# Written order for the transfer queue behind a router, and a new interleaving of two token tiles

## The chip, the cores and the metric

The kernel runs on one core of a Trainium2 chip. The metric is the device time of one execution in microseconds (us). Engines that work beside each other are PE (TensorE, matrix products), DVE (VectorE), ACT (ScalarE), POOL (GpSimd) and SP (SyncE), which here issues nearly all transfers. An engine executes its instructions in the order in which they stand in its queue; a wait of one holds up those behind it. Transfers that SP has issued are carried out by 16 DMA engines.

## What is computed

One layer on 256 tokens of 1024 values: two kinds of attention on the same modulated input, merged by sigmoid gates, an output projection, a layer norm, then a mixture of 32 experts of which each token uses four, and a second layer norm. Cut to the part around the change:

```python
x = layer_norm(DEEPNORM_ALPHA * x + gate1 * (merged @ w_out[l]), ln1_g[l], ln1_b[l])
h = x * (1.0 + scale2) + shift2
logits = jnp.dot(xt, w_router) + b_router
top_val, top_idx = lax.top_k(logits, TOP_K)
top_w = jax.nn.softmax(top_val, axis=-1)
# for each expert e, on the tokens that chose it:
g = jnp.minimum(xb @ w_gate[e] + b_gate[e], SWIGLU_LIMIT)
up = jnp.clip(xb @ w_up[e] + b_up[e], -SWIGLU_LIMIT, SWIGLU_LIMIT)
y = ((up + 1.0) * (g * jax.nn.sigmoid(SWIGLU_ALPHA * g))) @ w_down[e] + b_down[e]
x = layer_norm(DEEPNORM_ALPHA * x + gate2 * f, ln2_g[l], ln2_b[l])
```

Each expert has three weight matrices of 1024 x 1024 f32 (4 MB each), and all 32 are read.

## The kernel before

The tokens lie in two tiles (t = 0, 1) of 128; a row of 1024 values is worked on in two halves (hf = 0, 1). After attention and merging, the part around the change is the output projection and the router, written as one hand-ordered section (`order_cm`, all engines but POOL): inside it each engine executes in the order of the source.

The steps of that section: `o_part(t, hf, i)` is half i of the output projection for tile t and half hf, 12 matmuls (each product in three terms); `resid` adds the residual on DVE and takes statistics; `r_T` transposes on PE and copies on ACT; `logits(t, hf)` adds eight matmuls to the router's logits; `mod_sums` makes the column sums `gsum` and `bsum` (one PE product with `wrsum`, two DVE operations), which `route` needs; `stats` makes mean and inverse deviation; `normalise(t, hf)` writes the normalised tile `xn`; `route(t)` takes the four best experts and writes `mask_bf`; `count(t)` counts on PE each expert's tokens up to each token; `place(t)` makes from that the selection matrix `pt0` of the first experts; `gather_first(t)` gathers their tokens by 8 matmuls per tile into two PSUM banks (tile sxg), which `evacuate` copies to SBUF; `weigh` makes the weights of the four experts.

Behind it stands a second section (`pe_cm`), hand-ordered for PE alone; the order of all other engines, SP among them, is a planner's, which works with a timeline of its own. In it `expert_group` runs 14 times: first group s, with two fixed experts (30 and 31), then e0 to e12, which hold the other 30 experts sorted by how many tokens chose them (two experts each in e0 to e3 and e8 to e12, three each in e4 to e7). A group makes gate (tiles sg, e0g, ...), up (su, e0u, ...) and down (sd, e0d, ...), each in eight steps k. Inside group s, `sort_a`, `sort_b` and `sort_c` sort the experts and write their numbers to `order_i`. At the head of each of e0 to e12, `nc.sync.value_load(order_i[...])` (L1442) loads the numbers of its experts into SP's registers, two or three loads, with which the addresses of that group's weights are made.

Space sets when a transfer can be issued. The 24 weight pieces of the fixed experts (1 MB each, L805) go to 20 blocks; `al` hands out the block that was given back longest ago. 11 of the 24 are issued in the first section, 13 by `fixed_w` in group s. Then 18 of the blocks become 9 pairs of 2 MB (`open_pairs`, in the order of `PLACES`: blocks 10 and 8, 1 and 2, 0 and 12, 13 and 16, 11 and 7, 4 and 14, 5 and 15, 6 and 9, 17 and 3), and each transfer of e0 to e12 (L1126) takes the pair that was given back longest ago. `give_back` follows every second step k of a product. By `al` and `fr`, the fixed gate's last quarter lies in blocks 10 and 8; the four quarters of up lie in 1 and 2, 0 and 12, 13 and 16, 11 and 7; the first quarter of down in 4 and 14, and its last piece in block 3, which held the fixed gate's third quarter.

Of the kernel before, what the change touches and what calls it, by code (L numbers as in the profile page):

```python
# [13 lines left out]
AF = mybir.ActivationFunctionType  # L14
ALU = mybir.AluOpType
# [58 lines left out]
def tile_layer(  # L74
# [31 lines left out]
    V, A, G, T, SP = nc.vector, nc.scalar, nc.gpsimd, nc.tensor, nc.sync  # L106
# [26 lines left out]
    def al(dt=F32, stay=False):  # L133

        some = [i for i in freed if i in STAY] if stay else []
        some = some or [i for i in freed if stay_open[0] or i not in STAY]
        assert some, "no block is free"
        i = min(some, key=freed.get)
        del freed[i]
        clock[0] += 1  # L140
        v = first.pop(i, None)
        if v is None or dt != F32:
            v = (aw if i in STAY else ar).tile([P, BLK], dt, tag=f"blk{i}", bufs=1, name=f"blk{i}_{clock[0]}")
        return v, i

    def fr(*blocks):
        for i in blocks:
            clock[0] += 1
            assert i not in freed
            freed[i] = clock[0]  # L150

    def ps_a(name):
        return ps_t("A", 4, name)

    def ps_b(name):
        return ps_t("B", nb[0], name)
# [5 lines left out]
    def rsqrt_neg(v, eps, pool, name):  # L162

        y = pool.tile([P, 1], F32, tag="rsy", bufs=2, name=f"{name}y")
        u = pool.tile([P, 1], F32, tag="rsu", bufs=2, name=f"{name}u")
        V.tensor_scalar_add(v, v, eps)
        V.tensor_scalar(y.bitcast(I32), v.bitcast(I32), -0.5, 1597463007.0, op0=ALU.mult, op1=ALU.add)
        for c3 in (3.0, 12.0, 768.0):
            V.scalar_tensor_tensor(u, y, v, y, op0=ALU.mult, op1=ALU.mult)
            V.scalar_tensor_tensor(y, u, c3, y, op0=ALU.subtract, op1=ALU.mult)  # L170
        return y
# [103 lines left out]
    for j in range(4):  # L275
        ps = ps_b(f"xT{j}")
        for kk in range(2):
            for t in range(2):
                k = 2 * j + kk
# [4 lines left out]
    def mm3(o, sh, sl, mh, ml, first, last):  # L284
        T.matmul(o, sh, mh, start=first, stop=False)  # L285
        T.matmul(o, sh, ml, start=False, stop=False)  # L286
        T.matmul(o, sl, mh, start=False, stop=last)  # L287
# [406 lines left out]
    for i in range(4):  # L694
        ahead(2)
        if i % 2 == 0:
            v, r = al()
# [81 lines left out]
    def mod_sums():  # L779
        ps = ps_b("gb")  # L780
        T.matmul(ps[:, 0:2 * E], ones_p, wrsum, start=True, stop=True)
        V.tensor_copy(gsum, ps[:, 0:E])
        V.tensor_add(bsum, ps[:, E:2 * E], br_b)


    engines = {e.engine for e in (T, A, V, G, SP)}
# [12 lines left out]
    def load_fixed(n):  # L799

        for _ in range(n):
            kind, kq, j = fixed_todo.pop(0)
            v, r = al(stay=kind == 0)
            v = v.rearrange("p (k n) -> p k n", k=2)
            SP.dma_start(v, rows_of(weights[kind], E - 2 + j)[:, 2 * kq:2 * kq + 2, :])  # L805
            fixed[kind][0][j].append(v)
            fixed[kind][1][j].append(r)
# [73 lines left out]
    st6, mv, y3, lgps = [], [], [], []  # L881
# [2 lines left out]
        st6.append(p3.tile([P, 4, 6], F32, tag="lnst", bufs=2, name=f"ln1st{t}"))  # L884
    po = {}

    def o_part(t, hf, i):
        ts = slice(t * P, (t + 1) * P)
        if i == 0:
            po[t, hf] = ps_a(f"o{t}_{hf}")  # L890
        hi, lo = WO[2 * hf + i][0:2]
        for kk in range(4):
            k = 4 * i + kk
            mm3(po[t, hf], mgh[:, k, ts], mgl[:, k, ts], hi[:, kk, :], lo[:, kk, :], k == 0, k == 7)

    def resid(t, hf):
        for q in range(2):
            sl = slice(hf * 512 + q * 256, hf * 512 + (q + 1) * 256)
            V.tensor_mul(r[:, t, sl], po[t, hf][:, q * 256:(q + 1) * 256], gate1[:, sl])
            V.scalar_tensor_tensor(r[:, t, sl], x_sb[:, t, sl], ALPHA, r[:, t, sl], op0=ALU.mult, op1=ALU.add)  # L900
        for q in range(2):
            sl = slice(hf * 512 + q * 256, hf * 512 + (q + 1) * 256)
            V.bn_stats(st6[t][:, 2 * hf + q, :], r[:, t, sl])

    def r_T(t, hf):
        for q in range(2):
            ps = ps_b(f"rT{t}_{hf}_{q}")
            k = 4 * hf + 2 * q
            for kk in range(2):
                T.transpose(ps[:, kk * P:(kk + 1) * P], r[:, t, (k + kk) * P:(k + kk + 1) * P], ident)  # L910
            A.copy(rT[:, k:k + 2, :].rearrange("p a n -> p (a n)"), ps[:, 0:2 * P])

    def logits(t, hf):
        if hf == 0:
            lgps.append(ps_b(f"lg{t}"))
        for k in range(4 * hf, 4 * hf + 4):
            T.matmul(lgps[t][:, 0:E], rT[:, k, :], wrs[:, k, 0, :], start=(k == 0), stop=(k == 7))

    def stats(t):
        m = p3.tile([P, 2], F32, tag="lnmv", bufs=2, name=f"ln1mv{t}")  # L920
        V.bn_aggr(m, st6[t])
        mv.append(m)
        y3.append(rsqrt_neg(m[:, 1:2], LN_EPS, p3, f"ln1rs{t}"))
        nb_ = p3.tile([P, 1], F32, tag="lnnb", bufs=2, name=f"lnnb{t}")
        V.tensor_scalar(nb_, m[:, 0:1], y3[t], -1.0, op0=ALU.mult, op1=ALU.mult)
        nbs.append(nb_)

    nbs = []

    def normalise(t, hf):  # L930
        v = xn[:, t, :, :].rearrange("p k q -> p q k")[:, 64 * hf:64 * hf + 64, :]
        src = r[:, t, hf * 512:(hf + 1) * 512].rearrange("p (q k) -> p q k", k=8)
        if t == 0 or hf == 1:
            A.activation(v, src, AF.Identity, bias=nbs[t], scale=y3[t])
        else:
            V.tensor_scalar(v, src, y3[t], nbs[t], op0=ALU.mult, op1=ALU.add)

    m8s, ohs = [], []

    def route(t):  # L940
        lg = p3.tile([P, E], F32, tag="lg", bufs=2, name=f"lgs{t}")
        V.scalar_tensor_tensor(lg, gsum, mv[t][:, 0:1], lgps[t][:, 0:E], op0=ALU.mult, op1=ALU.subtract)
        V.scalar_tensor_tensor(lg, lg, y3[t], bsum, op0=ALU.mult, op1=ALU.add)
        m8 = p3.tile([P, 8], F32, tag="m8", bufs=2, name=f"m8_{t}")
        V.max(m8, lg)
        i8 = p3.tile([P, 8], U32, tag="i8", bufs=2, name=f"i8_{t}")
        V.max_index(i8, m8, lg)
        oh = p3.tile([P, 4, E], F32, tag="oh", bufs=2, name=f"oh{t}")
        V.tensor_tensor(oh, iota_e.unsqueeze(1).to_broadcast([P, 4, E]),
                        i8[:, 0:4].unsqueeze(2).to_broadcast([P, 4, E]), op=ALU.is_equal)  # L950
        V.tensor_reduce(mask_bf[:, t, :], oh.rearrange("p j e -> p e j"), axis=AX.X, op=ALU.max)
        m8s.append(m8)
        ohs.append(oh)
# [3 lines left out]
    def count(t):  # L957
        cum[t] = ps_b(f"cum{t}")
        if t == 1:
            T.matmul(cum[t][:, 0:E], ones_bf, mask_bf[:, 0, :], start=True, stop=False)  # L960
        T.matmul(cum[t][:, 0:E], tri, mask_bf[:, t, :], start=(t == 0), stop=True)

    def place(t):
        V.tensor_mul(posm[:, t, :], cum[t][:, 0:E], mask_bf[:, t, :])
        V.tensor_tensor(pt0[:, t, :].rearrange("p (a n) -> p a n", a=2),
                        iota_s[:, 0:CAP].unsqueeze(1).to_broadcast([P, 2, CAP]),
                        posm[:, t, E - 2:E].unsqueeze(2).to_broadcast([P, 2, CAP]), op=ALU.is_equal)
# [31 lines left out]
            else:  # L999
                V.tensor_scalar(xg[:, k, :], src, gc[:, k:k + 1], bc[:, k:k + 1], op0=ALU.mult, op1=ALU.add)  # L1000

    def gather_first(t):
        if t == 0:
            for i in range(2):
                gps.append(ps_a(f"sxg{i}"))
                T.matmul(gps[i], zero_bf, zero_bf.unsqueeze(1).to_broadcast([P, 4, P]), start=True, stop=False, skip_group_check=True)
        for k in range(8):
            T.matmul(gps[k // 4][:, (k % 4) * P:(k % 4 + 1) * P], xn[:, t, k, :], pt0[:, t, :], start=False, stop=(t == 1),
                     skip_group_check=True)

# [4 lines left out]
    for i in range(2):  # L1015
        for t in range(2):
            o_part(t, 0, i)
        fr(*WO[i][2:4])
        if i == 0:
            split_wo()  # L1020
        else:
            mod_sums()
        load_fixed(2)
    for t in range(2):
        resid(t, 0)
# [1 line left out]
        o_part(0, 1, i)  # L1027
    r_T(0, 0)
    logits(0, 0)
    resid(0, 1)  # L1030
    o_part(1, 1, 0)
    fr(*WO[2][2:4])
# [3 lines left out]
    stats(0)  # L1036
    for hf in range(2):
        normalise(0, hf)
    o_part(1, 1, 1)
    fr(*WO[3][2:4])  # L1040
    route(0)
    count(0)
    resid(1, 1)
    r_T(1, 1)
    for hf in range(2):
        logits(1, hf)
    place(0)
    gather_first(0)
    stats(1)
    normalise(1, 1)  # L1050
    route(1)
    normalise(1, 0)
    count(1)
    place(1)
    gather_first(1)
    evacuate(xg0, gps)
# [323 lines left out]
        if i < len(GROUPS):  # L1380
            tokens[i] = gather(f"e{i}", group_slots(i))

    pe_cm = tc.manual_schedule(engines={T.engine})
    pe_cm.__enter__()
    expert_group("s", segments((64, 64)), gather("s", None), lambda t, j: wtok[:, t, E - 2 + j:E - 1 + j], fixed_w,
                w_bias(sel0.rearrange("p a n -> p (a n)")), {("g", 0): sort_a, ("g", 3): sort_b, ("g", 7): sort_c},
# [134 lines left out]
```

## Time and profile before

| | us |
|---|---|
| median of 3 runs | 1211.18 |
| lowest and highest of them | 1209.35, 1215.85 |
| the profiled execution | 1212.23 |
| its span, first to last instruction | 1210.5 |
| PE busy in it | 1049.7 (87%) |
| DVE, ACT, POOL busy | 372.6, 176.3, 96.8 |
| mean rate of the transfers | 384 GB/s, 464.55 MB |

The profile is of one execution. A row of a timeline gives start, length, engine, line, operation, tiles and shapes, and in brackets how long the engine had been idle and what ended that. SP's rows are issues of transfers, which take a third of a microsecond; the transfer itself lands later. A share of 1.00 of the DMA engines means that all 16 were at work.

### The profile page before, as it was taken

The page shows a single profiled execution, that of the slowest core. Times are in us where ns is not written, and L with a number is a line of the kernel's source. Part 1 is how long each engine was busy: PE and PEld are TensorE (multiplying, and loading weights), DVE is VectorE, ACT ScalarE, POOL GpSimd, SP SyncE. Part 2 cuts the span into 40 slices and gives each one's busy share as a digit, 9 for nine tenths or more (in the row PEclk, how much of TensorE's full clock was granted, in tenths as well). Part 3 has the DMA queues.
Part 4 walks back from the last instruction along what each step waited for, and adds up shares of the span by engine and source line. Part 5 has one row for each costly group of instructions (what it writes and reads, how often), then busy time and mean ns, then how long its engine had stood idle before and what let it go on. Part 6 is the DMA issues. An engine that isn't in the chain of part 4 may idle for free.

```text
span 1210.5 us, 18672 instructions
## 1 busy us (share of the span) xinstructions
PE 1049.7 (87%) x7991; PEld 475.7 (39%) x7991; DVE 372.6 (31%) x751; ACT 176.3 (15%) x363; POOL 96.8 (8%) x120
## 2 busy tenths in 40 slices
PE   6889899889999999997768868868779898989895
PEld 4668788754343323332212312312324242424231
DVE  4777995864112112211101101101102030303024
ACT  3346554321000000000000000000000000101001
POOL 2121555300000000000000000000000000000000
PEclk8889999999999999998888888889889999999998
DMA  9968657997999999999999999999999999999992
GB/s 338 328 214 296 244 197 246 365 416 290 426 425 428 425 426 426 427 426 427 426 429 425 428 426 426 428 427 426 427 427 426 426 424 428 426 427 426 426 400 79
DMA packets 68204, 464.55 MB, mean 384 GB/s; under 512 B 8698, under 2 KB 33319, under 8 KB 39959
## 3 DMA queue, kind: packets, MB, share of 16 engines
q1 hardware_dynamic: 67830, 462.28, 93.2%
q8 instruction: 64, 1.05, 0.3%
q10 hardware_dynamic: 288, 1.05, 0.3%
q14 instruction: 22, 0.17, 0.0%
HBM read 462.24 MB, written 1.06 MB: 383 GB/s over the span
## 4 chain that ended last, share of the span: by engine, by line
DMA 48%; PE 40%; DVE 5%; SPq 2%; ACT 2%; issue 1%; POOL 1%; DVEq 0%; ACTq 0%; POOLq 0%
DMA wt<-in_w_gate_dram 21%; DMA wt<-in_w_up_dram 20%; DMA wt<-in_w_down_dram 5%; PE e12d L1172 1%; PE e11d L1172 1%; PE e0d L1172 1%; PE sd L1172 1%; PE e1u L1172 1%; PE e0u L1172 1%; PE e1g L1172 1%; PE e0g L1172 1%; PE e2u L1172 1%; PE su L1172 1%; DMA blk<-in_b_down_dram 1%; DVE blk L649 1%
## 5 line engine op out<-in xcount | busy, mean ns | idle before, releaser
L1215 ACT ACTIVATE blk<-blk 128x512 f32<-128x512 f32 x28 | 17.2, 630 | 532.4 <-DVE blk L1213 532.3
L160 POOL TENSOR_TENSOR blk<-blk,blk 128x512 fp32r<-128x512 f32 (+2 forms) x44 | 82.6, 1896 | 146.5 <-ACT blk L159 89.5
L1446 POOL COPY sel<-sel 96x64 bf16<-96x64 bf16 (+2 forms) x30 | 5.9, 231 | 832.4 <-PE e6d L1263 88.7
L159 ACT CAST blk<-blk 128x512 fp32r<-128x512 f32 (+2 forms) x76 | 53.7, 767 | 38.9 <-DVE blk L862 12.2
L160 DVE TENSOR_TENSOR blk<-blk,blk 128x512 fp32r<-128x512 f32 (+2 forms) x32 | 39.6, 1244 | 20.7 <-ACT blk L159 16.3
L649 DVE SCALAR_TENSOR_TENSOR blk<-blk,csil,blk 128x1024 f32<-128x1024 f32 x28 | 40.4, 1476 | 1.0 <-DMA blk<-in_w_ada_dram 0.9
L287 PE MATMUL g<-blk,blk 128*128 128x256 f32 x128 | 37.3, 294 | 1.8 <-POOL blk L160 1.4
L285 PE MATMUL g<-blk,blk 128*128 128x256 f32 x128 | 37.5, 293 | 0.2 <-ACT blk L159 0.2
L286 PE MATMUL g<-blk,blk 128*128 128x256 f32 x128 | 37.2, 291 | 0.0
L1172 PE MATMUL e6g<-wt,xgb 128*32 128x512 f32 x128 | 20.6, 734 | 9.0 <-DMA wt<-in_w_gate_dram 9.0
L1172 PE MATMUL e7g<-wt,xgb 128*32 128x512 f32 x128 | 21.4, 745 | 7.9 <-DMA wt<-in_w_gate_dram 7.7
L1172 PE MATMUL e4g<-wt,xgb 128*32 128x512 f32 x128 | 20.7, 748 | 8.5 <-DMA wt<-in_w_gate_dram 8.5
L1172 PE MATMUL e5g<-wt,blk 128*32 128x512 f32 x128 | 19.5, 694 | 7.7 <-DMA wt<-in_w_gate_dram 7.7
L287 PEld LDWEIGHTS g<-blk,blk 128*128 128x128 f32 x128 | 24.9, 196 | 3.1 <-POOL blk L160 2.2
L286 PEld LDWEIGHTS g<-blk,blk 128*128 128x128 f32 x128 | 25.1, 196 | 1.2 <-issue 1.2
L285 PEld LDWEIGHTS g<-blk,blk 128*128 128x128 f32 x128 | 25.2, 197 | 0.8 <-ACT blk L159 0.5
L1172 PE MATMUL e6u<-wt,xgb 128*32 128x512 f32 x128 | 19.7, 691 | 6.5 <-DMA wt<-in_w_up_dram 6.5
L1172 PE MATMUL e5u<-wt,blk 128*32 128x512 f32 x128 | 19.3, 699 | 6.9 <-DMA wt<-in_w_up_dram 6.9
L1172 PE MATMUL e4u<-wt,xgb 128*32 128x512 f32 x128 | 19.5, 696 | 6.5 <-DMA wt<-in_w_up_dram 6.5
L1172 PE MATMUL e7u<-wt,xgb 128*32 128x512 f32 x128 | 19.7, 694 | 6.3 <-DMA wt<-in_w_up_dram 6.3
L1172 PE MATMUL e5d<-wt,blk 128*32 128x512 f32 x128 | 18.2, 661 | 6.9 <-DMA wt<-in_w_down_dram 6.5
L1172 PE MATMUL e4d<-wt,xgb 128*32 128x512 f32 x128 | 17.8, 655 | 5.6 <-DMA wt<-in_w_down_dram 5.4
(738 smaller groups left out, 1844.0 us busy)
## 6 DMA issues: line engine op xcount, KB each, us to landing
wt<-in_w_gate_dram SPq DMA_DIRECT2D x60, 2048.0 KB, 30.4
wt<-in_w_up_dram SPq DMA_DIRECT2D x60, 2048.0 KB, 30.3
wt<-in_w_down_dram SPq DMA_DIRECT2D x58, 2048.0 KB, 32.9
blk<-in_w_ada_dram SPq DMA_DIRECT2D x24, 1024.0 KB, 8.8
blk<-in_w_in_dram SPq DMA_DIRECT2D x12, 1024.0 KB, 5.3
blk<-in_w_gate_dram SPq DMA_DIRECT2D x8, 1024.0 KB, 8.0
blk<-in_w_up_dram SPq DMA_DIRECT2D x8, 1024.0 KB, 13.7
blk<-in_w_down_dram SPq DMA_DIRECT2D x8, 1024.0 KB, 10.0
```

What stands on the lines that cost most here:

```text
L159: A.copy(hi, src)
L160: (V if eng == "V" else G).tensor_sub(lo, src, hi.bitcast(F32))
L285: T.matmul(o, sh, mh, start=first, stop=False)
L286: T.matmul(o, sh, ml, start=False, stop=False)
L287: T.matmul(o, sl, mh, start=False, stop=last)
L649: eng.scalar_tensor_tensor(acc_v[:, sl], v[:, q * D:(q + 1) * D], csil[:, k:k + 1], acc_v[:, sl], op0=ALU.mult, op1=ALU.add)
L1172: T.matmul(pss[hf][c0:c0 + m, :], stat[:, k, c0:c0 + m], ch[par][k // 2][:, k % 2, hf * 512:(hf + 1) * 512], start=(k == 0), stop=(fine an ...
L1215: A.activation(s, g[:, sl], AF.Sigmoid, scale=SW_ALPHA)
L1446: G.tensor_copy(sel[:, lo:lo + n], sel96[:, r:r + 1].to_broadcast([96, n]))
```

## The change

In the second section SP is put into the order of the source as PE is (`engines={T.engine, SP.engine}`). In the first section the order of steps is written anew: `mod_sums` moves behind `logits(0, 0)`; `route(0)` comes ahead of the last `o_part`, and `count(0)` goes between its ninth and its last three matmuls (argument `mid`); `place(0)` stands ahead of `resid(1, 1)`; `logits(1, 0)` ahead of `r_T(1, 1)`; `gather_first(0)` is cut into 2, 5 and 1 of its 8 matmuls, between which stand `logits(1, 1)`, `stats(1)`, both halves of `normalise(1)`, `route(1)` and `count(1)`. All of `normalise` is now on ACT; before, half 0 of tile 1 was on DVE.

```diff
-    def o_part(t, hf, i):
+    def o_part(t, hf, i, mid=None):
...
             mm3(po[t, hf], mgh[:, k, ts], mgl[:, k, ts], hi[:, kk, :], lo[:, kk, :], k == 0, k == 7)
+            if mid is not None and kk == 2:
+                mid()
...
-        if t == 0 or hf == 1:
-            A.activation(v, src, AF.Identity, bias=nbs[t], scale=y3[t])
-        else:
-            V.tensor_scalar(v, src, y3[t], nbs[t], op0=ALU.mult, op1=ALU.add)
+        A.activation(v, src, AF.Identity, bias=nbs[t], scale=y3[t])
...
-    def gather_first(t):
-        if t == 0:
+    def gather_first(t, ks=range(8)):
+        if t == 0 and 0 in ks:
...
-        for k in range(8):
+        for k in ks:
...
         fr(*WO[i][2:4])
         if i == 0:
             split_wo()
-        else:
-            mod_sums()
         load_fixed(2)
...
     r_T(0, 0)
     logits(0, 0)
+    mod_sums()
     resid(0, 1)
...
-    o_part(1, 1, 1)
+    route(0)
+    o_part(1, 1, 1, lambda: count(0))
     fr(*WO[3][2:4])
-    route(0)
-    count(0)
+    place(0)
     resid(1, 1)
+    logits(1, 0)
     r_T(1, 1)
+    gather_first(0, range(2))
+    logits(1, 1)
+    stats(1)
+    gather_first(0, range(2, 7))
     for hf in range(2):
-        logits(1, hf)
-    place(0)
-    gather_first(0)
-    stats(1)
-    normalise(1, 1)
+        normalise(1, hf)
     route(1)
-    normalise(1, 0)
     count(1)
+    gather_first(0, range(7, 8))
     place(1)
     gather_first(1)
...
-    pe_cm = tc.manual_schedule(engines={T.engine})
+    pe_cm = tc.manual_schedule(engines={T.engine, SP.engine})
```

## Rows read from the trace of the kernel before

**Rows 1.** The page's slices, 30.3 us each: what the DMA engines moved.
```profile
GB/s 338 328 214 296 244 197 246 365 416 290 426 425 428 425 426 426 427 426 427 426 429 425 428 426 426 428 427 426 427 427 426 426 424 428 426 427 426 426 400 79
```

**Rows 2.** Table by stage: stretch, length, each engine's busy time, clock, DMA share, GB/s.
```profile
236.00:276.00 40.00, 36.21 (x247) 24.09 (x250) 25.52 (x94) 8.77 (x19) 0.23 (x1) 0.93 1.01 418
276.00:282.00 6.00, 6.00 (x70) 2.79 (x66) 2.04 (x7) 0.63 (x1) 0.86 (x4) 1.00 0.99 348
282.00:284.00 2.00, 2.00 (x24) 0.66 (x20) 2.00 (x7) 0.63 (x1) 0.00 (x0) 1.00 0.52 205
284.00:290.00 6.00, 6.00 (x64) 2.09 (x60) 6.00 (x4) 0.00 (x0) 0.00 (x0) 1.00 0.00 1
290.00:292.00 2.00, 2.00 (x24) 0.70 (x20) 0.14 (x1) 0.00 (x0) 0.00 (x0) 1.00 0.58 123
292.00:400.00 108.00, 107.49 (x947) 39.78 (x940) 22.97 (x45) 8.05 (x16) 0.42 (x2) 1.00 1.01 426
400.00:1165.00 765.00, 653.37 (x4985) 222.09 (x4988) 124.41 (x255) 44.40 (x88) 4.61 (x24) 0.92 1.01 426
```

**Rows 3.** The chain that ended last, two links: start, length, what.
```profile
300.10 13.94 PE sd L1172 x128
...
399.16 33.42 DMA wt<-in_w_gate_dram
```

**Rows 4.** Timeline of SP, 270 to 330 us, then 303.0 to 304.2: issues of transfers.
```profile
270.03 6.22 SPq L805 DMA_DIRECT2D blk<-in_w_down_dram  x3
289.92 2.11 SPq L1126 DMA_DIRECT2D wt<-in_w_gate_dram  x4
294.91 16.09 SPq L1126 DMA_DIRECT2D wt<-in_w_up_dram  x4
...
303.80 0.33 SPq L1126 DMA_DIRECT2D wt<-in_w_up_dram  x1
```

**Rows 5.** Line 1442 alone: ns min/median/max, first and last start in us.
```profile
L1442 SPq TENSOR_LOAD <-order_i x30: 261/265/474, 271.6 to 289.1; - x30
```

**Rows 6.** Timeline of PE, 271 to 296 us: second half of sg, then su.
```profile
271.85 7.07 PE L1172 MATMUL sg<-blk,xgb 128*32 128x512 f32 x64
...
280.94 13.93 PE L1172 MATMUL su<-blk,xgb 128*32 128x512 f32 x127
```

**Rows 7.** Issues in 247.0:248.6 and in 329.0:329.4: KB, median us to landing.
```profile
blk<-in_w_up_dram SPq DMA_DIRECT2D x2, 1024.0 KB, 11.3
...
wt<-in_w_gate_dram SPq DMA_DIRECT2D x1, 2048.0 KB, 28.6
```

**Rows 8.** Timeline of PE in the router section.
```profile
235.13 0.69 PE L781 MATMUL gb<-wrsum,ones_p 128*128 128x64 f32 x2 [2.36 <-DVE wrsum L777]
...
243.37 1.08 PE L917 MATMUL lg<-wrs,xgb 128*128 128x32 f32 x8 [0.24 <-ACT xgb L911]
...
247.13 0.60 PE L910 MATMUL rT<-ident,blk 128*128 128x128 f32 x4
...
260.87 2.02 PE L1008 MATMUL sxg<-pt,xn 128*128 128x128 f32 x16 [0.73 <-DVE pt L965]
```

**Rows 9.** Timelines of DVE and, last row, of ACT in the router section.
```profile
235.00 2.30 DVE L160 TENSOR_TENSOR blk<-blk,blk 128x1024 fp32r<-128x1024 f32 x1
...
242.72 0.42 DVE L899 TENSOR_TENSOR blk<-o,gate 128x256 f32<-128x256 f32 x1 [0.73 <-PE o L287]
...
249.09 0.25 DVE L942 SCALAR_TENSOR_TENSOR lgs<-gsum,ln1mv,lg 128x32 f32<-128x32 f32 x1 [1.76 <-PE lg L917]
...
250.51 0.39 DVE L951 TENSOR_REDUCE mask_bf<-oh 128x32 bf16<-128x128 f32 x1
...
258.83 0.72 DVE L936 TENSOR_SCALAR xn<-blk,ln1rs1y,lnnb 128x512 f32<-128x512 f32 x1
...
249.93 2.38 ACT L934 ACTIVATE xn<-blk,lnnb,ln1rs0y 128x512 f32<-128x512 f32 x2
```

**Rows 10.** Table by stage, granted clock (third from the right) behind that pause of PE.
```profile
235.10:238.40 3.30, 3.27 (x9) 2.69 (x10) 3.27 (x6) 0.00 (x0) 1.12 (x1) 0.50 1.01 427
```

## The prediction

> **What bounds the kernel now.** I began with the whole run. From the eleventh slice on, the row of GB/s stays at 424 to 429 nearly to the end, while the tenth slice has 290 [rows 1]. So the second part of the kernel, thirteen expert groups that stream 2 MB weight blocks, runs at the rate of the transfers. The stage table confirms it: 426 GB/s with the 16 DMA engines at a share of 1.01 from 292 to 1165 us, and 418 at 1.01 from 236 to 276 [rows 2]. Between these two saturated stretches lies a hole: 205 GB/s in 282 to 284, 1 GB/s in 284 to 290, 123 in 290 to 292 [rows 2]. The bytes are the same whatever is done, so a hole in the stream is lost time.
>
> The chain of waits tells it otherwise. It goes through the router, the first experts on PE (the down part of expert group s at 300.10, for instance) and only at 399.16 turns into a transfer that takes 33.42 us to land [rows 3]. It takes the issue of that transfer for its cause. But 33.42 us is no price of one 2 MB transfer (4.9 us at 426 GB/s); nearly all of it is queueing behind the blocks issued earlier. So what counts there is how early the queue was filled, hence the hole, not when PE released that one block.
>
> **Why the hole is there.** The last transfer of the fixed experts is issued at 275.91 (three issues from 270.03, the last ending at 276.25), and the first of group e0 at 289.92 [rows 4]. In between SP does one thing: 30 register loads of `order_i` (L1442), from 271.6 to 289.1 [rows 5]. That is 17.5 us between first and last, 0.57 us apart with the one transfer in between. These are the expert numbers of all 13 groups (4 x 2 + 4 x 3 + 5 x 2 = 30): the planner put them all ahead of e0's first transfer, though in the source each group's two or three stand right before that group's own loads.
>
> Were e0's blocks free earlier? Following `al` and `fr` through the source, weight pair 0 covers blocks 10 and 8 (last quarter of the fixed gate weights), pairs 1 to 4 the quarters of the fixed up weights, pair 5 the first quarter of down. Each comes free when PE has passed that quarter. The second half of sg runs from 271.85 to 278.92, su from 280.94 to 294.87 in four equal quarters, sd from 300.10 [rows 3, 6]. So the pairs were free at 278.9, 284.4, 287.9, 291.4 and 294.9. They were asked for at 289.92, 290.5, 291.1, 291.7 and 294.91 [rows 4]: the fifth issue falls on its release, which supports this reading, and the first came 11.0 us late.
>
> **The change part by part.**
> 1. *SP in written order.* SP does two register loads (1.1 us) behind the last fixed transfer instead of 30. That transfer is free at 275.4 (half of the second half of sg [rows 6]), so SP stands at pair 0 by about 277 and waits for 278.9, well before the queue runs dry at 282. Pair 0 gives 4.9 us of work, to 287.9; pair 1, free at 284.4, carries it to 292.8; the next follow with more room. The hole closes: 2 x (426-205)/426 = 1.04, 6 x 425/426 = 5.99 and 2 x (426-123)/426 = 1.42, together **8.45 us** [rows 2]. I count nothing for 276 to 282: its 348 GB/s has a share of 0.99, the engines are busy there [rows 2]; were that a hole too, it would be 1.1 more.
> 2. *Is the next wait late?* The sixth transfer waits for sd's first quarter and is issued at 303.80 [rows 3, 4]. With the stream closed, what is left of the fixed loads (205 GB/s for 2 us [rows 2]) ends at 283.0 and the five ahead of it at 283.0 + 5 x 4.92 = 307.6. Less the 1.0 us from an issue to its first bytes (estimated from the issue at 289.92 and a flow of only 123 GB/s in 290 to 292 [rows 2, 4]) this leaves a margin of 2.8 us even if PE is no earlier. Later ones have more: the transfer issued at 329.07 takes 28.6 us to land [rows 7].
> 3. *The 28 register loads that move.* They now stand at 12 group boundaries, 2 or 3 each, 1.1 to 1.7 us of SP. Queued behind them is the next gate transfer; who waits for that is PE, 28.6 us later [rows 7]. Cost zero under that cover; 28 x 0.57 = 16 us if it were gone. The Trainium skill speaks against spreading them: "DMA: Bandwidth & Descriptors", Latency and other measured facts, gives a floor of about 600 ns for a tensor load and has the compiler unroll four of them to amortise it. By that, single loads could cost more than bunched ones. The trace shows the bunched ones at 0.57 us apart, so nothing was amortised [rows 5], and the sum stays as it is.
> 4. *mod_sums behind logits(0,0).* PE no longer idles 2.36 us until 235.13 for `wrsum` [rows 8], nor runs the next 3.3 us at the lower clock (granted 0.50 [rows 10]) for that reason. The first half of output part (0,1) runs from 232.8 and takes 2.7 us (247.13 less 244.45, the same work between two rows [rows 8]). Its second half then waits for the split of the last weights on DVE, which ends at 237.30 [rows 9], and is done at 240.0, or 241.2 if this shorter pause drops the clock too; before, 242.7 [rows 9]. Logits(0,0) and the sum matmul follow, 0.65 + 1.08 + 0.69 at most [rows 8, 9]. DVE must wait for them: `gsum` and `bsum` now stand ahead of resid(0,1), which starts at 242.3 to 243.9 instead of 242.72. A new wait that eats half of the gain.
> 5. *The rest of the router.* r_T(0,1) at 244.8 to 246.4 instead of 247.13, because output part (1,1) begins earlier; route(0) as much earlier than 249.09. Count(0) stands inside the last output part, nine matmuls (2.0 us) in, when the mask, written 1.8 us after route(0) begins (249.09 to 250.90 [rows 9]), is just there. The first half of token tile 1's logits goes into the time in which PE waited for resid(1,1), saving another 1.1 [rows 8]; its PSUM tile is then alive beside cum(0) and two transposes, which fills the four buffers of that kind, but place(0) gives cum(0) back ahead of resid(1,1). Gather_first(0) is cut into pieces of 2, 5 and 1 with the same instructions. The DVE half of normalise(1), 0.72 at 258.83, becomes an ACT half beside DVE's route(1); two ACT halves cost 2.38 [rows 9]. In all gather_first(1) starts at 257.6 to 259.1 instead of 260.87: 1.8 to 3.3 us earlier.
> 6. *What 4 and 5 are worth.* Nothing by themselves. From 236 to 283 the transfers are saturated, and loads that wait for this stage have 11.3 us from issue to landing [rows 7]; an earlier PE only widens the margin of step 2. If the stage came out longer instead, it would cost nothing up to about 3 us (278.9 against 282), and each further us fully.
>
> **Sum.** The profiled execution took 1212.23 us (span 1210.5), the median of the runs shown is 1211.18, 1.05 lower. Less 8.45: 1203.8 for a profiled execution, **1202.7** for the median.
>
> **The rivals.**
> - *The chain is right* (or the register loads stay bunched in the new program): only the router counts, since the loads of `order_i`, and with them the hole, move with it. 1.8 to 3.3 us, take 2.5: 1208.7. For it: every row of the chain before 399.16 is PE. Against it: the queueing time of 33.42 us [rows 3]. Chance 0.10.
> - *Part of the hole returns.* Sd's first quarter or su's come late by more than the 2.8 us of step 2, through planner choices on DVE or ACT, or the router loses time. 2 to 4 us come back: 1205 to 1207. For it: the margin is thin at just that place. Chance 0.13.
> - *Slower: the register loads show.* If the queue ran empty at group boundaries, 12 pauses of 1.1 to 1.7 us add 16 us against 8.45 won: 1219. It decides at a backlog under 1.7 us; the row has 28.6 [rows 7]. Chance 0.04.
> - *More is won*: the slow stretch of 276 to 282 tightens as well, 1.1 us: 1201.6, inside the forecast's spread. Chance 0.05.
>
> **How the numbers follow.** The forecast keeps 0.68. The runs shown spread from 1209.35 to 1215.85, so a median can lie some 2 us off, and the forecast's own range is 1200 to 1205.5. With the chain's rival in and most of the gain of a tighter start, the range is 1199.5 to 1208.7. About 0.5% (6.1 us, below 1205.1) is what a measurement can tell from no change. Faster: the forecast, the better case and a little of the partial one, less what noise takes, 0.73. Same: 0.22. Slower: 0.05.
>
> **What would show it.** Right: no stretch under 400 GB/s between 284 and 292; the first gate transfer of e0 issued at 276 to 279 instead of 289.92; `order_i` loads spread to about 1085; SP waiting for sg and su quarters between its first transfers; the stream's end some 8 us earlier; gather_first(1) near 258. Wrong: a hole again around 304 to 309 (step 2), a group boundary without backlog (step 3), or a shift of the whole stream by only the router's 2.5 us.

## The result, and the profile after

The changed kernel takes **1204.64 us** (median of 10 runs, 1202.43 to 1208.28) against 1211.43 for the kernel before, timed beside it (10 runs). The ratio is 0.9945, with an interval from 0.9931 to 0.9959: 5.0 to 8.4 us are gone, 6.8 by the medians. The forecast was 8.45 us and 1202.7. The profiled execution took 1207.04, of which the span is 1205.3.

The slices of the page after, which answer to [rows 1]; from the ninth on the row is at 420 or more, but for its last two, and the tenth, 290 before, is at 424:
```profile
GB/s 334 324 210 294 263 182 249 349 420 424 427 424 426 426 425 425 430 424 425 427 427 426 428 425 427 426 427 426 429 426 424 425 427 426 426 428 426 425 376 59
```
The table by stage after, with the columns of [rows 2] (stretch, length, busy time of PE, weight loads, DVE, ACT and POOL, granted clock, DMA share, GB/s):
```profile
236.00:276.00 40.00, 35.62 (x257) 21.79 (x259) 26.43 (x94) 9.88 (x20) 1.60 (x1) 0.96 1.01 420
276.00:282.00 6.00, 6.00 (x70) 2.86 (x66) 3.76 (x12) 1.26 (x2) 0.86 (x4) 1.00 1.03 421
282.00:284.00 2.00, 2.00 (x24) 0.66 (x20) 1.11 (x2) 0.00 (x0) 0.00 (x0) 1.00 1.00 420
284.00:290.00 6.00, 6.00 (x64) 2.09 (x60) 4.36 (x4) 0.00 (x0) 0.00 (x0) 1.00 1.01 428
290.00:292.00 2.00, 2.00 (x24) 0.70 (x20) 1.14 (x2) 0.00 (x0) 0.00 (x0) 1.00 1.02 434
```
The hole of 282 to 292 is gone, and a stretch that had not been counted as one moved too: 276 to 282 carries 421 GB/s instead of 348. At 426 GB/s the differences to [rows 2] are worth 0.19 (236 to 276), 1.03, 1.01, 6.01 and 1.46, together **9.7 us**.

SP's issues after, which answer to [rows 4] (start, length, line, out and in, count):
```profile
277.26 0.36 SPq L1125 DMA_DIRECT2D wt<-in_w_gate_dram  x1
282.89 0.33 SPq L1125 DMA_DIRECT2D wt<-in_w_gate_dram  x1
...
293.19 0.34 SPq L1125 DMA_DIRECT2D wt<-in_w_up_dram  x1
...
302.34 0.33 SPq L1125 DMA_DIRECT2D wt<-in_w_up_dram  x1
```
The loads of `order_i`, one line higher in the changed program ([rows 5] before; count, ns min/median/max, first and last start):
```profile
L1441 SPq TENSOR_LOAD <-order_i x30: 262/268/488, 274.2 to 1084.7; - x30
```
And SP's waits for the loads of e0 from 274 to 304 us after (engine, line, for whom: us in total, times, longest):
```profile
SPq L1125 <- PE su L1171: 10.8, 3, 5.0
SPq L1125 <- PE sd L1171: 8.2, 1, 8.2
...
SPq L1125 <- PE sg L1171: 1.4, 1, 1.4
```
The first transfer of e0 goes out at 277.26 instead of 289.92, and all that SP's transfers of e0 wait for there is now PE: quarters of sg, of su, of sd. The 30 loads lie where the source has them.

The router after, on PE, then on DVE and ACT ([rows 8, 9]; start, us, engine, line, out and in, count, idle time before and its releaser):
```profile
238.74 0.50 PE L286 MATMUL o<-blk,blk 128*128 128x512 f32 x1 [1.67 <-DVE blk L160]
...
243.13 0.41 PE L781 MATMUL gb<-wrsum,ones_p 128*128 128x64 f32 x2
...
258.78 2.69 PE L1007 MATMUL sxg<-pt,xn 128*128 128x128 f32 x16 [0.39 <-DVE pt L964]
```
```profile
236.40 2.29 DVE L160 TENSOR_TENSOR blk<-blk,blk 128x1024 fp32r<-128x1024 f32 x1
...
243.58 0.19 DVE L782 COPY gsum<-gb 128x32 f32<-128x32 f32 x1 [0.40 <-PE gb L781]
243.78 0.41 DVE L901 TENSOR_TENSOR blk<-o,gate 128x256 f32<-128x256 f32 x1
...
256.18 2.28 ACT L935 ACTIVATE xn<-blk,lnnb,ln1rs1y 128x512 f32<-128x512 f32 x2 [2.01 <-DVE lnnb L927]
```
The split that everything here follows ends at 238.69 instead of 237.30 [rows 9]: this execution came into the section 1.4 us late, ahead of all that was changed. In spite of it gather_first(1) starts at 258.78 instead of 260.87.

The chain after, with [rows 3] beside it (start, length, what):
```profile
298.64 13.94 PE sd L1171 x128
...
450.08 32.88 DMA wt<-in_w_gate_dram
```
It still goes through PE up to a transfer that it takes 32.88 us to land. The chain has hardly changed its look, though what bounds the kernel there, the hole, is gone.

Last, PE in the last group, **the kernel before** and then after:
```profile
1145.05 7.06 PE L1172 MATMUL e12g<-wt,xgb 128*32 128x512 f32 x60 [2.72 <-DMA wt<-in_w_gate_dram]
...
1156.69 15.05 PE L1172 MATMUL e12u<-wt,xgb 128*32 128x512 f32 x128
...
1175.64 3.60 PE L1237 MATMUL e12c<-x_sb,ident 128*128 128x512 f32 x8
```
```profile
1137.75 8.45 PE L1171 MATMUL e12g<-wt,xgb 128*32 128x512 f32 x60 [4.05 <-DMA wt<-in_w_gate_dram]
...
1150.77 13.94 PE L1171 MATMUL e12u<-wt,xgb 128*32 128x512 f32 x128
...
1167.62 1.85 PE L1229 MATMUL e12hT<-ident,blk 128*128 128x128 f32 x8 [2.37 <-DVE blk L1221]
1169.26 4.62 PE L1236 MATMUL e12c<-x_sb,ident 128*128 128x512 f32 x8
```
Here the two profiled executions lose part of the gain again. The last 60 products of e12g start 7.3 us earlier than before but take 8.45 us instead of 7.06; e12u gives 1.1 back; the eight of e12c take 4.62 instead of 3.60 and end 5.4 us earlier than before (1173.88 against 1179.24). So the ledger of the profiled pair is 9.7 won in the stream, 1.4 lost ahead of the change, about 3 lost in the last group, 5.2 left in the span. Counted by the packets of the two traces it is the same: 455 of the 464.55 MB have been moved by 1161.8 us before and by 1153.5 after, 8.3 earlier; from there to the end of the span it is 48.7 us before and 51.8 after. This last stretch is called the tail below. Whether the last two losses belong to the change was for the runs to say.

### The profile page after: what moved, and what is told of

It reads as the page before. It is cut to its first block, busy times and chain, and to the rows that moved or that the text cites. A ratio compares the mean times of both kernels' runs of the same rounds, so it can differ in the third digit from the quotient of the medians.

```text
span 1205.3 us, 18673 instructions
## 1 busy us (share of the span) xinstructions
PE 1045.2 (87%) x7991; PEld 476.0 (39%) x7991; DVE 372.5 (31%) x750; ACT 177.2 (15%) x364; POOL 96.6 (8%) x120
## 2 busy tenths in 40 slices
DMA packets 68203, 464.55 MB, mean 385 GB/s; under 512 B 8697, under 2 KB 33318, under 8 KB 39958
## 4 chain that ended last, share of the span: by engine, by line
DMA 41%; PE 39%; DVE 3%; ACT 2%; issue 1%; SPq 0%; POOL 0%; DVEq 0%; ACTq 0%
DMA wt<-in_w_gate_dram 22%; DMA wt<-in_w_up_dram 14%; DMA wt<-in_w_down_dram 3%; PE sg L1171 1%; PE e2u L1171 1%; PE e8u L1171 1%; PE e12d L1171 1%; PE e10d L1171 1%; PE e1d L1171 1%; PE e0d L1171 1%; PE e9d L1171 1%; PE sd L1171 1%; PE e12u L1171 1%; PE e2g L1171 1%; PE e1u L1171 1%; PE e0u L1171 1%
## 5 line engine op out<-in xcount | busy, mean ns | idle before, releaser
L1171 PE MATMUL e7d<-wt,xgb 128*32 128x512 f32 x128 | 19.5, 684 | 6.2 <-DMA wt<-in_w_down_dram 5.9
```

The lines of the kernel that those rows point to most:

```text
L1171: T.matmul(pss[hf][c0:c0 + m, :], stat[:, k, c0:c0 + m], ch[par][k // 2][:, k % 2, hf * 512:(hf + 1) * 512], start=(k == 0), stop=(fine an ...
```

## The experiments

**The theory**: the stream sets the time, and the hole in it was the only thing that the change removed, by the order of SP; the router alone is worth nothing once the hole is closed. **The rivals**: the chain of waits is right and the router carries the gain; the register loads between groups cost something that the profile hides; the last group takes back part of the gain.

### SP's order alone

```diff
# the kernel before
-    pe_cm = tc.manual_schedule(engines={T.engine})
+    pe_cm = tc.manual_schedule(engines={T.engine, SP.engine})
```


> Only SP is put into written order; the router stands as before. Theory of the stream: the hole of 282 to 292 us closes although the router is no shorter, because the first pairs are free at 278.9, 284.4 and 287.9 whatever the order; the gain is that of the whole change, a ratio of about 0.9945 (1204.7), no stretch under 400 GB/s between 284 and 292, first gate transfer of e0 issued near 279. Theory of the chain (only the router on PE counts before 399 us): no gain, ratio 1.000.

1204.77 us in the median of 6 runs (before: 1211.9 in 23); ratio 0.9935, from 0.9917 to 0.9953. SP's issue and the table by stage of this kernel:
```profile
277.69 12.83 SPq L1126 DMA_DIRECT2D wt<-in_w_gate_dram  x4
```
```profile
276.00:282.00 6.00, 6.00 (x70) 2.85 (x66) 3.32 (x11) 1.26 (x2) 0.86 (x4) 1.00 1.01 411
...
284.00:290.00 6.00, 6.00 (x64) 2.10 (x60) 3.98 (x2) 0.00 (x0) 0.00 (x0) 1.00 1.03 434
```
One word in the source gives as much as the whole change (0.9945), with the router of the kernel before untouched. By the chain's theory this kernel should have been close to the kernel before. (The word fixes all of SP's order in that section, not the place of the register loads alone; that is for e3.) It also closes the stretch of 276 to 282.

### The router alone

```diff
# the changed kernel
-    pe_cm = tc.manual_schedule(engines={T.engine, SP.engine})
+    pe_cm = tc.manual_schedule(engines={T.engine})
```


> Only the router section is new; SP's order is left to the planner, which again puts 30 register loads ahead of e0's first transfer. Theory of the stream: the hole stays some 8 us long and only moves with the router, 2 to 3.4 us earlier; ratio 0.997 to 0.9985 (1208 to 1209.5). Theory of the chain: the router is the cause, the whole gain is here, ratio 0.9945 (1204.7).

1210.89 us in 12 runs; ratio 0.9988, from 0.9975 to 1.0. Its loads of `order_i`, SP's first issue for e0, and its table by stage:
```profile
L1441 SPq TENSOR_LOAD <-order_i x30: 260/266/472, 268.1 to 285.6; - x30
```
```profile
286.41 2.11 SPq L1125 DMA_DIRECT2D wt<-in_w_gate_dram  x4
```
```profile
282.00:284.00 2.00, 2.00 (x24) 0.75 (x20) 2.00 (x2) 0.00 (x0) 0.00 (x0) 1.00 0.10 41
284.00:290.00 6.00, 6.00 (x64) 2.10 (x56) 3.54 (x3) 0.00 (x0) 0.00 (x0) 1.00 0.44 139
```
The 17.5 us block of loads is back, 3.5 us earlier than in [rows 5], and the hole with it. So the new order of the router does move the block, as the rival says, but what arrives of it is 0 to 3 us, 1.0 by medians, a little less than was expected.

### The bunched loads on their own

```diff
# the changed kernel
+    all_ids = [[nc.sync.value_load(...) for r, _ in group] for group in GROUPS]
...
-        ids = [nc.sync.value_load(...) for r, _ in group]
+        ids = all_ids[i]
```


> The changed kernel, SP in written order, but the 30 register loads are written in one block ahead of e0's first transfer. If these loads are the cause, the hole comes back: first gate transfer of e0 at about 291 instead of 277.3, 6 to 9 us without transfers, ratio 0.9975 to 1.000 (1208.4 to 1211.4). If another part of SP's written order is the cause (which piece of the fixed weights goes first, say), the ratio stays near 0.9945 and no hole is seen.

1214.68 us in 12 runs; ratio 1.0019, from 1.0005 to 1.0033. Loads, first issue and stage of this kernel:
```profile
L1439 SPq TENSOR_LOAD <-order_i x30: 260/266/485, 273.3 to 290.3; - x30
```
```profile
291.12 2.11 SPq L1125 DMA_DIRECT2D wt<-in_w_gate_dram  x4
```
```profile
284.00:290.00 6.00, 6.00 (x64) 2.09 (x59) 4.90 (x4) 0.00 (x0) 0.00 (x0) 1.00 0.01 3
```
This keeps everything of the change but the place of the register loads, and the whole gain is gone, and more than the expected 0.9975 to 1.000: the first transfer goes out at 291.12, 1.2 us later than in the kernel before [rows 4], and the tail is 51.2 us, 2.5 longer than before. This is the cause shown, and from both sides: e1 takes the block away without the router, this run puts the block alone back.

### Four times the register loads at every boundary

```diff
# the changed kernel
+        for _ in range(3):
+            for r, _n in group:
+                nc.sync.value_load(order_i[0:1, r:r + 1], min_val=0, max_val=E - 1)
         ids = [nc.sync.value_load(...) for r, _ in group]
```


> The changed kernel with every register load done four times in its group: 8 or 12 loads, 4.5 to 6.8 us of SP, at each of the 12 group boundaries, and 4.5 us ahead of e0. Theory of the cover (a gate transfer waits some 28 us in the queue anyway): no change, ratio 0.994 to 0.996. Rival, that register loads of SP show at the boundaries: three extra sets add 90 x 0.57 = 51 us, ratio about 1.037 (1256); half of that if half is hidden.

1204.82 us in 6 runs; ratio 0.9937, from 0.9917 to 0.9957, where e1 has 0.9935. The 90 added loads of this kernel:
```profile
L1443 SPq TENSOR_LOAD <-order_i x90: 261/267/492, 272.9 to 1085.4; - x90
```
Ninety more loads, 51 us of SP at 0.57 each, cost nothing that can be seen. The cover of step 3 holds, with room. The floor for single tensor loads that the Trainium skill gives ("DMA: Bandwidth & Descriptors", Latency and other measured facts) is of the size seen here, 0.57 us each. Where transfers are queued ahead, this kernel pays nothing for it. The unrolling by four that the Trainium skill names there is not what the planner did, and no run here tests it; gathering 30 loads left them 0.57 us apart and put them ahead of a transfer [rows 5].

### The last group: a clock that falls

In the profile after, PE pauses 4.05 us for the last gate weights and 2.37 us for DVE, and the work behind each pause is slow. Four kernels ask whether that belongs to the change. The first is the changed kernel once more, for the comparison on one chip.

> The changed kernel once more, beside the next three and for a second profile of its last group. Theory of the tail: the stream runs about 8.4 to 9.7 us earlier than before, but in the last group PE no longer waits for transfers alone; it pauses for the second half of the gate weights and for DVE ahead of the transposes e12hT, the clock it is granted falls to 0.50 in some of these pauses, and 1.5 to 3 us of the stream's gain are lost there. Ratio 0.994, and the time from the stream's 455th MB to the end 50 to 51.5 us, against 48.3 in the profile of before. Rival: the shorter gain is scatter of the runs; the stretch is near 48.3 us again in about half of the profiles, of this kernel too.

1204.18 us in 7 runs; ratio 0.9936, from 0.9913 to 0.9958. PE in its last group:
```profile
1136.74 8.57 PE L1171 MATMUL e12g<-wt,xgb 128*32 128x512 f32 x60 [4.18 <-DMA wt<-in_w_gate_dram]
...
1168.26 4.73 PE L1236 MATMUL e12c<-x_sb,ident 128*128 128x512 f32 x8
```
The tail is 51.9 us by the same count that gives 48.7 for before, and 50 to 51.5 was expected of a loss there: the short tail did not come back. In the next, PE is kept busy through both pauses with products that nobody reads:
```diff
# the changed kernel
+    def fill(nm, n):
+        ps = ps_b(f"{nm}fill")
+        for _ in range(n):
+            T.matmul(ps, ones_bf[0:96, :], bias3[0][:, 0:512], start=True, stop=True)
...
+        if end is not None:
+            fill(nm, 10)
...
-                     ... {("g", 0): items_a, ("g", 2): items_b, ("g", 5): items_c} if i == 3 else {},
+                     ... {("g", 0): items_a, ("g", 2): items_b, ("g", 5): items_c} if i == 3
+                     else {("g", 3): lambda: fill("e12g", 12)} if last else {},
```


> The changed kernel with filling on PE in the last group alone: 12 products of 0.21 us whose result nobody reads between the steps 3 and 4 of e12's gate, and 10 of them ahead of e12hT, where PE waits anyway. No work is taken away. Theory of the tail (the clock falls in these pauses): no granted clock of 0.50 between e12g and e12d, 1.5 to 3 us faster than the changed kernel, ratio 0.9915 to 0.993. Rival (scatter): no gain, ratio 0.994, or a little slower if the filling is in the way.

1202.71 us in 6 runs; ratio 0.9915, from 0.9891 to 0.9938. PE in its last group:
```profile
1136.73 7.06 PE L1176 MATMUL e12g<-wt,xgb 128*32 128x512 f32 x60 [0.42 <-DMA wt<-in_w_gate_dram]
...
1167.29 3.60 PE L1243 MATMUL e12c<-x_sb,ident 128*128 128x512 f32 x8
```
The same 60 products that took 8.57 us behind a pause of 4.18 in the repeated run take 7.06 with the filling, and the eight of e12c 3.60 instead of 4.73. The granted clock tells why; two microseconds behind the first pause, in the repeated run and then with the filling (table by stage, clock third from the right):
```profile
1137.00:1139.00 2.00, 2.00 (x12) 0.39 (x8) 0.00 (x0) 0.00 (x0) 0.00 (x0) 0.50 1.02 434
```
```profile
1137.00:1139.00 2.00, 2.00 (x24) 0.62 (x20) 0.00 (x0) 0.00 (x0) 0.00 (x0) 1.00 1.00 426
```
At 0.50, which is 1.2 GHz, 12 products are done in the time of 24. Not all of that is kept: e12u takes 15.03 us with the filling and 13.94 without, at a granted clock of 1.00 in both, and the tail comes to 50.0 us. The medians are 1.5 us apart, and the intervals of the two ratios overlap. Then the same filling in the kernel before:

> The kernel before with the same filling in its last group. Its profile shows no fall of the clock there, so by the theory of the tail it gains little: ratio 0.9985 to 1.0005. If the fall of the clock in the last group comes as often before as after the change, it gains as much as the other one, 0.9975 to 0.9985, and the tail explains nothing of the difference between stream and time.

1210.64 us in 12 runs; ratio 0.9982, from 0.9966 to 0.9999, whose middle is what equal falls would give and whose ends reach into the other theory. The filling gains 1.5 us after and 1.5 before, by medians. If that is the clock's, the clock falls in the last group of the kernel before as well. Its own profile shows no fall there, but e2, with SP's order left to the planner as before, does, behind a pause of the same length as that of the kernel before (2.72 us, e12g in 7.06):
```profile
1141.58 8.76 PE L1171 MATMUL e12g<-wt,xgb 128*32 128x512 f32 x60 [2.72 <-DMA wt<-in_w_gate_dram]
```
Its granted clock is 0.50 from 1143 to 1145. So the fall does not need the closed hole, and behind the same pause it comes in one execution and not in another. That the loss at the end is no cost of the change is **not shown**, though. The tails are 48.7 us before, 49.4 in e2 and 48.9 in e7, all with the planner's order, and 51.2 to 52.3 in all seven profiles with SP in written order and nothing done to the last group (after, e1, e3, e4, the repeated run, e11, e12). And e7's profile is 2.2 us shorter than that of before because its stream is 2.4 us earlier, not because of its tail. What in the written order would make the tail longer, no run tells.

One more lets useful work do the filling: half of e12c ahead of e12hT, and the add-up of e11 inside the gate part of e12.
```diff
# the changed kernel
+        def start_po(hf):
+            for t in range(2):
+                po[t, hf] = ps_b(f"{nm}c{t}_{hf}")
+                T.matmul(po[t, hf], ident, macc[:, t, hf * 512:(hf + 1) * 512], start=True, stop=False)
+        if end is not None:
+            start_po(0)
...
+                     else {("g", 3): give_add} if last else {},
```


> The changed kernel with useful work in the two pauses: the products that start the output sums for the first half (four of the eight of e12c) ahead of e12hT, and the adding up of e11 between the steps 3 and 4 of e12's gate, both of them done later before. By both theories the wait for DVE ahead of e12hT (2.37 us) now hides 1.8 us of e12c, so 1.8 us are won: ratio 0.9925. By the theory of the tail the clock stays up as well and e12's up part starts 3.6 us earlier where transfers allow: 2.5 to 4.5 us won, ratio 0.9905 to 0.992.

1203.19 us in 6 runs; ratio 0.9921, from 0.9897 to 0.9945, which does not tell the theories apart. The moved work left a gap where it had stood, in e12u:
```profile
1153.93 8.76 PE L1171 MATMUL e12u<-wt,xgb 128*32 128x512 f32 x60 [2.73 <-DMA wt<-in_w_up_dram]
```
The fall of the clock only changed its place (granted 0.50 from 1154 to 1156). The best of both, filling of 12 products in the gate part, then 3 and the first half of e12c ahead of e12hT:
```diff
# the changed kernel, with fill and start_po as above
+        if end is not None:
+            fill(nm, 3)
+            start_po(0)
...
+                     else {("g", 3): lambda: fill("e12g", 12)} if last else {},
```


> The changed kernel with the filling in e12's gate pause as in e6_fill_after, and ahead of e12hT four of the eight products of e12c (useful, 1.8 us) with three fillings in front. It should take e6_fill_after's gain, the granted clock staying at 1.00 from e12g to e12d, and start e12d some 1.6 us earlier: ratio 0.990 (about 1201). If the clock is not what costs time in the last group, it gains the 1.6 us alone: ratio 0.992.

1202.27 us in 6 runs (1200.1 to 1203.73), beside 1211.33 for the kernel before; ratio 0.9927, from 0.9914 to 0.9941. It is the lowest median of all, though e6 and e9 have lower ratios (0.9915 and 0.9921) to the kernel before beside them; against the changed kernel (0.9936 and 0.9945) the intervals overlap, so its own share, 2 us by medians, isn't settled to better than that. The 0.990 that was expected isn't reached.

### How late the router may be

Step 6 said that some 3 us of delay in front of sg would be free. Unread products on PE, ahead of the first expert group:
```diff
# the changed kernel
+    hold = ps_b("hold")
+    for _ in range(19):            # 47 in the second kernel
+        T.matmul(hold, zero_bf, zero_bf.unsqueeze(1).to_broadcast([P, 4, P]), start=True, stop=True)
```


> The changed kernel with 19 products that nobody reads (4.05 us on PE) between gather_first(1) and the first gate product of group s, so that this group comes some 2 to 3 us later. Theory of the stream: the queue had 4.5 to 5 us of margin (the second pair's transfer is issued at 282.9, and the one ahead of it ends near 288.4), so nothing is lost: ratio as of the changed kernel, 0.9935 to 0.9945. Theory of the chain: every microsecond of the router counts, 2 to 3 us lost, ratio 0.996.

1205.83 us in 5 runs; ratio 0.9957, from 0.9944 to 0.997. The table by stage:
```profile
236.00:276.00 40.00, 36.98 (x271) 22.26 (x275) 23.93 (x93) 9.77 (x20) 0.00 (x0) 1.00 1.00 413
276.00:282.00 6.00, 6.00 (x70) 2.85 (x66) 3.69 (x12) 1.26 (x2) 0.86 (x4) 1.00 0.99 339
```
The 19 products take 4.26 us, of which part goes into a pause that sg had anyway: from the end of the split on DVE (236.25 here, 237.67 in the repeated run) to the second half of sg (270.20, 268.77) it is 33.95 us instead of 31.1 (31.4 in the profile after), so the delay that counts is 2.85 at most. Against after's table the stream loses 0.66 + 1.15 = 1.8 us of it, in 236 to 276 and in 276 to 282. The medians are 1.65 us apart (1204.18), with overlapping intervals. The ratio is the 0.996 that was written down for the chain, not the 0.9935 to 0.9945 of the stream. Some 1 us was free, not 3.

> The same with 47 such products, 10 us on PE, so that group s comes 8 to 9 us later. Theory of the stream: the margin of 4.5 to 5 us is used up and the rest is lost, 3 to 4 us, ratio about 0.997, with a stretch of low GB/s near 290 or 312. Theory of the chain: 8 to 9 us lost, ratio 1.001.

1212.8 us in 12 runs; ratio 1.0014, from 1.0004 to 1.0024: the whole gain is lost. That again is the number of the chain's theory (1.001), not the 0.997 of the stream, and the thin stretch is not near 290 or 312. The table by stage, and SP's issues:
```profile
236.00:276.00 40.00, 37.29 (x239) 23.26 (x237) 21.77 (x88) 9.88 (x20) 0.00 (x0) 0.96 0.84 343
276.00:282.00 6.00, 6.00 (x59) 1.85 (x60) 0.68 (x1) 0.00 (x0) 0.00 (x0) 1.00 0.93 351
```
```profile
272.22 7.97 SPq L805 DMA_DIRECT2D blk<-in_w_down_dram  x4
283.33 12.83 SPq L1128 DMA_DIRECT2D wt<-in_w_gate_dram  x4
```
By the same count the second half of sg is 10.5 us late (234.57 to 276.19), and 8.6 us of that are in the median. The first transfer of e0 goes out at 283.33, about when the queue was to have run dry, but the stream is thin before that: (420 - 343) x 40 / 426 = 7.2 us are missing from 236 to 276. What comes late are the last four **fixed** down loads, issued over 272.22 to 280.19 (after: 266.16 to 274.13, in an execution that came into the section 4.1 us later). They wait for quarters of sg, stand ahead of e0's transfers in SP's order, and the queue has nothing else. Step 6 looked at the margin of e0's transfers and passed over these. So both theories have a share: the loss is seen in the stream, but a later router makes it, all but the first 1 to 2 us of the delay. An earlier router gives nothing that can be seen (e1 against the whole change).

## Why the prediction was right, and where it was off

**The bound and the cause** (the first two parts): right. The chain of waits and the stream said different things, and e1, e2 and e3 decide for the stream: with the block of register loads gone the gain is there without the new router, and with the block alone put back it is gone.

**Step 1**: the transfer foreseen for 276 to 279 goes out at 277.26, and waits for sg as said. The hole gave 8.48 (1.01 + 6.01 + 1.46) for a forecast of 8.45. The mis-sized term is the one that was set to nothing: 276 to 282 gave 1.03 more. The share of 0.99 there [rows 2] was taken for full engines. The queues in 276 to 280, **the kernel before** and then after (packets, MB, share of the 16 engines), show what differs:
```profile
q10 hardware_dynamic: 143, 0.52, 51.4%
q1 hardware_dynamic: 107, 0.75, 46.5%
```
```profile
q1 hardware_dynamic: 170, 1.26, 76.0%
q10 hardware_dynamic: 94, 0.39, 23.6%
```
A second queue, q10, carries the two broadcast loads that ACT issues for the first layer norm. Before, its packets took 51.4% of the engines for 0.52 MB; after, 23.6% for 0.39 MB, with more weights moving beside them (1.26 MB for 0.75). A share near 1 stands for 339 to 434 GB/s in the tables here. Why the same packets take longer when the weight queue is short isn't settled by a run; e11 shows 339 GB/s at 0.99 with e0's transfer already issued, so it isn't that transfer's issue time alone.

So the rival "more is won" (chance 0.05) is what the stream did: 9.7 us, not 8.45. That the time came out 1.9 us above the forecast instead of below has another term. The sum let each microsecond of the stream be one of the time, and so put the tail behind the stream at no change. In the profiles the tail is 48.7 us before and 51.2 to 51.9 in after, e1, e4, the repeated run and e11, 2.5 to 3.2 longer; 9.7 less that is 6.5 to 7.2, where the medians have 6.8 (the result), 7.1 (e1) and 8.0 (the repeated run). Part of the longer tail is the clock, 8.45 us for e12g instead of 7.06 and 4.62 for e12c instead of 3.60 in the profile after; part is the longer pause, 4.05 us instead of 2.72, for the last gate weights. Whether and why these come with SP's written order **stays open**: only two profiles (before and e2) have both the planner's order and an untouched last group. The 1.4 us ahead of the change belong to that one execution (the split that ends at 238.69 there and at 237.30 before ends at 237.67 in the repeated run). That the forecast lies within 2 us of the result is thus in part luck: it left out about 1.2 us more in the stream and about 3 us less at the end, and these have opposite signs.

**Step 2**: the sixth transfer goes out at 302.34 (303.80 before), and from 304 to 309 the profile after has 413 GB/s at a share of 0.98, 0.15 us short. The margin was enough; the rival of a returning hole did not come.

**Step 3**: right, by e4 with room to spare. The transfer that stands first at e1's boundary lands 20.2 us after its issue at 328.79; before, 28.6 [rows 7]. The backlog shrank and still covers loads of 0.57 us.

**Step 4**: with the 1.4 us of this execution taken off, the second half of output part (0,1) ends at 240.1 (forecast 240.0 to 241.2; the clock did not fall behind the pause of 1.67, its products start 0.23 apart), and resid(0,1) starts at 242.4 (242.3 to 243.9). `gsum` stands ahead of it and is released by PE, the new wait that was named.

**Step 5**: gather_first(1) at 258.78, or 257.4 with the 1.4 us off, for a forecast of 257.6 to 259.1; the two ACT halves of normalise(1) take 2.28 for 2.38.

**Step 6**: its first half is right: parts 4 and 5 add nothing to SP's order (e1 0.9935, the change 0.9945 and 0.9936). Its second half is wrong. "Up to about 3 us" of delay free was worked out for e0's first transfer (278.9 against 282). The nearest work that hangs on sg is the fixed down loads ahead of it: of 2.85 us of delay e11 lost 1.65 by medians, of 10.5 e12 lost 8.6. So 2 us at most are free, and what lies beyond costs in full, as the step said of its own margin.

## What to carry to other kernels

When a stream of transfers sets the time, look for the stretch in which the bytes per time fall, and read what the issuing queue did just before: small blocking instructions that a planner gathers in front of a transfer cost nothing among queued transfers, and ahead of a queue that runs dry whatever the queue does not cover (here 7 to 10 of 17.5 us). A chain of waits that ends in a transfer of many times its own length is showing a queue, not a cause. What the stream gains still has to come through the work behind it: here 9.7 us became 6.8, so compare the tails too. And a margin belongs to the first thing in the queue's order that depends on the late work, not to the one whose wait was looked at.

## What the runs showed of the hardware

- A DMA share of 0.99 went with 339, 348 and, at 1.03, with 421 GB/s in the same stretch: the share alone doesn't tell the rate.
- 120 register loads on SP in place of 30 cost nothing between queued transfers; 30 in a row cost 17.5 us of that queue, and 7 to 10 us of the kernel (e1 against before, e3 against e1).
- Behind pauses of 2.37 and 4.18 us TensorE was granted 0.50 in the repeated run, and 60 products took 8.57 us instead of 7.06; with products that nobody reads in those pauses it was 1.00 and 7.06 us. The medians are 1.5 us lower with them in either kernel, against the changed kernel with overlapping intervals.
- Behind a pause of 2.72 us the granted clock stayed at 1.00 in the profile of before (60 products in 7.06 us) and fell to 0.50 in that of e2 (8.76 us): the length of the pause alone does not tell.
